# A two-layer hybrid backbone on one core: the opening of the first layer regrouped into quarters, with identity transposes in TensorE's early waits

## The chip, the cores and the metric

The kernel runs on one core of one Trainium2 chip. The metric is the device time of one execution in microseconds (us). A core has TensorE (PE; its weight loads are listed apart as PEld), VectorE (DVE), ScalarE (ACT), GpSimd (POOL) and SyncE (SP), each with an instruction queue of its own that it works off in order, and 16 DMA engines that move data between memory and the on-chip buffers.

## The reference

There are 1024 latent tokens and 256 context tokens of width 1024, and two layers. Each layer normalizes the tokens, scales and shifts them by a modulation that is computed from a conditioning vector (one for the latent, one for the context tokens), mixes them, and adds the gated result. Layer 0 mixes by windowed attention with sink logits, layer 1 by multi-head latent attention.

```python
def adaln(cond, w, bias):
    m = jax.nn.silu(cond) @ w + bias
    return jnp.split(m, 3, axis=-1)
...
        shift_x, scale_x, gate_x = adaln(c, ada_w[i], ada_b[i])
        shift_c, scale_c, gate_c = adaln(c_ctx, ada_w[i], ada_b[i])
        hx = rms_norm(x, norm_g[i]) * (1.0 + scale_x[:, None]) + shift_x[:, None]
        hc = rms_norm(ctx, norm_g[i]) * (1.0 + scale_c) + shift_c
...
        q, k, v, g = jnp.split(h @ w_in, [A_WIDTH, A_WIDTH + A_KV_WIDTH, A_WIDTH + 2 * A_KV_WIDTH], axis=-1)
...
        x = x + gate_x[:, None] * yx
        if need_ctx:
            ctx = ctx + gate_c * yc
    return rms_norm(x, final_g)
```

All of it is float32. In `adaln` the first third of the columns is the shift and the second the scale; the gates are computed elsewhere in the kernel.

## The kernel before

Most products are made from operands cut into a high part (rounded to the format in which TensorE streams fastest) and a low part (the rest). `mm3` (lines 124 to 128) adds three matmuls: high by high, low by high, high by low; the profile has them as L126, L127 and L128. `split` (lines 119 to 122) makes the parts: ScalarE copies the high one (L121), another engine subtracts (L122).

The tokens lie in ten row tiles of 128, two context and eight latent tiles, handled as five pairs of 256 tokens. The **opening** (lines 657 to 864) makes the modulated input `hT` of layer 0, which all later projections read, and the first product from it, the values `V`, whose weights are block 0 (`w0`, 1024 x 256). Then a loop over the other blocks of the input projection begins (line 869), in an order written out by hand (`in_order`), then the attention, then layer 1.

The steps of the opening, by function:

- `ada_load(h, k)` loads modulation weights, 128 rows of a 512-column half `h` of shift and of scale (0.52 MB), into one of six buffers; `ada_mm(h, k)` (L676) makes two matmuls of 512 columns from them, for shift and scale. Eight `k` make a half. `ada_cols(h)` copies the two sums out of the bank (L679), turns them into columns (L681), and `set_cols` (L168, L171) adds the biases and forms the columns `A` (scale) and `B` (shift).
- `x_load(i)` loads a row tile (0.52 MB) into one of **four** buffers `xs`. `norm(i)` sums its squares on ScalarE (L692) and has GpSimd form the inverse root (L693, L694); `scale(i)` multiplies the tile by it (L701 on VectorE, L699 on ScalarE).
- A **group** is a pair `p` and a quarter `b` of the 1024 columns; there are 20. `turn(g)` (L712) makes four 128x128 transposes into a bank. `h_part(g)` has VectorE scale and shift them out of it (L723, two of 128x256) and ScalarE round the high half (L724, 128x512); `h_low(g)` subtracts for the low half (L729, on GpSimd or VectorE). The scaled group lies in one of four buffers `hr` until then. `v_part(g)` makes the group's twelve value matmuls, and at a pair's last quarter takes the values out of the bank (L745, L747).
- `w0_load` and `w0_cut` load and split quarters of block 0 of the weights; `fetch` (L288) does so for later blocks. `load_small` loads the identity `ident`, the modulation biases, the norm gains and the sink logits on ScalarE's queue, and VectorE negates the sinks (L151). All other loads are issued by SyncE.

Groups go in the order quarters 0 and 1 of pairs 0 and 1, then their quarters 2 and 3, then four quarters of each of pairs 2 to 4. The opening's order on each engine is the planner's, which sorts by priority and may let an instruction of a later stage go first; the stage behind it (`in_order`) is in program order.

Behind the opening, `ada_vec` computes the rest of the modulation on VectorE (L342, L344), step by step in the projection loop, and TensorE sums it over the rows (L355).

Of the kernel before, what the change touches and what calls it, by code (L numbers as in the profile page):

```python
# [9 lines left out]
F32 = mybir.dt.float32  # L10
# [8 lines left out]
D = 1024  # L19
# [8 lines left out]
F_KB = 66  # L28
# [31 lines left out]
def kernel(ctx: ExitStack, tc: tile.TileContext, t, out, dbg=None):  # L60
# [93 lines left out]
    class AdaLN:  # L154
# [8 lines left out]
        def set_cols(self, mt, what, h):  # L163

            l, j0 = self.layer, 8 * what + 4 * h
            bias = adab[:, l, j0 : j0 + 4].unsqueeze(2).to_broadcast([128, 4, 2])
            dst = (self.A if what else self.B)[:, 4 * h : 4 * h + 4]
            nc.vector.tensor_add(dst, mt, bias)  # L168
            if what:
                g = ng[:, l, 4 * h : 4 * h + 4].unsqueeze(2).to_broadcast([128, 4, 2])  # L170
                nc.vector.scalar_tensor_tensor(dst, dst, 1.0, g, ALU.add, ALU.mult)  # L171
# [108 lines left out]
    def fetch(bi):  # L280
# [9 lines left out]
        def cut(i):  # L290
            ks = slice(2 * i, 2 * i + 2)
            split(wt[bi][:, 0, ks, :], wt[bi][:, 1, ks, :], got[i], nc.gpsimd)
# [364 lines left out]
    awr = Ring(F, [0, 4, 8, 12, 16, 20], 1024)  # L657
    xs = Ring(F, [24, 28, 32, 36], 1024)
    w0r = Ring(F, [40, 42], 512)
    am = f_at(48, 512)  # L660
    junk = f_at(50, 512).bitcast(BF16)
    hr = Ring(F, [44, 46, 40, 42], 512)
    PA, PM = PB[:, 6, :], PB[:, 7, :]
    parts = [(p, b) for h in range(2) for p in range(2) for b in (2 * h, 2 * h + 1)]
    parts += [(p, b) for p in range(2, NP) for b in range(4)]
    NG = len(parts)
    aw, xn, hs, w0 = {}, {}, {}, {}

    def ada_load(h, k):
        aw[h, k] = shp(awr.next(), 2, 512)  # L670
        src = t["ada_w"][0, k * 128 : k * 128 + 128, 0 : 2 * D].rearrange("p (a c) -> p a c", a=2)
        load(out=aw[h, k], in_=src[:, :, h * 512 : h * 512 + 512])

    def ada_mm(h, k):
        for a in range(2):
            nc.tensor.matmul(PA[32 * a : 32 * a + 2], sc[:, k, :], aw[h, k][:, a, :], start=k == 0, stop=k == 7)  # L676

    def ada_cols(h):
        nc.scalar.copy(am[0:34], PA[0:34])  # L679
        for j in range(4):  # L680
            nc.tensor.transpose(PM[:, 34 * j : 34 * j + 34], am[0:34, j * 128 : j * 128 + 128], ident[0:34, 0:34])  # L681
        m = shp(PM, 4, 34)
        ada0.set_cols(m[:, :, 32:34], 1, h)
        ada0.set_cols(m[:, :, 0:2], 0, h)
# [962 lines left out]
```

## Time and profile before

| what | value |
|---|---|
| time, median of three runs | 1561.43 us (1560.34 to 1561.45) |
| time of the profiled execution | 1563.35 us |
| its span, first to last instruction | 1561.6 us |
| mean granted TensorE clock | 0.989 of full speed |
| moved by DMA | 178.91 MB, mean 115 GB/s |
| DMA share in the first ten microseconds / the next twenty | 0.72 / 1.05 |
| chain that ended last, share of PE | 86% |

A row of a group of instructions names the line in the kernel, the engine, the operation, what is written and read with its shape, how many there were, and times. A float32 matmul of the modulation counts as two records. Durations of matmuls overlap, so the distance from one start to the next says what one costs. In a list of waits the columns are total, times and longest in us. A row of one line of the kernel has the shortest, median and longest duration in ns, then the first and last start in us.

### The profile page before, as it was taken

The numbers are of one execution on the slowest core, as the hardware profiler recorded it, in microseconds if no ns is written. First come the engines' busy times: TensorE is split into PE (matmuls) and PEld (weight loads), VectorE is DVE, ScalarE is ACT, GpSimd is POOL, SyncE is SP. The second block draws the span as 40 slices with busy tenths as digits, with TensorE's granted clock in tenths as the row PEclk, the third lists the DMA queues.
The fourth block names the chain that finished last, engine by engine and source line by source line (L and its number), as shares of the span: only waits on it lengthen the run. The fifth ranks groups of instructions, "written<-read, shape, count | busy, mean of one in ns | idle before, by whom it ended". The sixth has DMA issues, their size and how long they took to land.

```text
span 1561.6 us, 24793 instructions
## 1 busy us (share of the span) xinstructions
PE 1513.9 (97%) x9074; PEld 1207.1 (77%) x9074; DVE 953.2 (61%) x1859; ACT 714.1 (46%) x1369; POOL 816.3 (52%) x764
## 2 busy tenths in 40 slices
PE   6899999999999999998999999999999999999998
PEld 2797888687888888887988788766876875885686
DVE  2666968827767787777826301556566566566644
ACT  2512212219877777776623332244443443453422
POOL 2652545417544443344517351278789789699200
PEclk8899999999999999999999999999999999999999
DMA  8425544474433322326304851402122112211442
GB/s 303 178 92 186 198 140 169 151 223 138 121 109 99 97 89 88 95 68 203 109 9 138 295 155 63 124 9 58 45 68 65 51 46 74 58 44 45 142 155 81
DMA packets 123986, 178.91 MB, mean 115 GB/s; under 512 B 11724, under 2 KB 72268, under 8 KB 123864
## 3 DMA queue, kind: packets, MB, share of 16 engines
q1 hardware_dynamic: 119032, 170.27, 34.8%
q10 hardware_dynamic: 4832, 7.06, 1.3%
q8 instruction: 71, 1.16, 0.3%
q14 instruction: 51, 0.42, 0.1%
HBM read 131.13 MB, written 46.15 MB: 114 GB/s over the span
## 4 chain that ended last, share of the span: by engine, by line
PE 86%; DMA 3%; DVE 3%; ACT 3%; issue 2%; POOL 2%; SPq 0%; POOLq 0%; DVEq 0%; ACTq 0%
PE PB L126 14%; PE PB L127 14%; PE PB L128 14%; PE PB L1345 12%; PE PB L1368 9%; PE PB L572 5%; PE PB L1311 5%; PE PB L562 4%; PE PB L532 2%; PE PB L533 2%; DMA arena_f<-a_w_in 1%; PE PB L1379 1%; DVE arena_f L344 1%; DMA arena_f<-b_w_in 1%; PE PB L355 1%
## 5 line engine op out<-in xcount | busy, mean ns | idle before, releaser
L126 PE MATMUL PB<-arena_r 128*128 128x512 f32 (+2 forms) x1312 | 477.2, 364 | 4.9 <-ACT arena_r L205 2.1
L127 PE MATMUL PB<-arena_r 128*128 128x512 f32 (+2 forms) x1312 | 470.0, 358 | 2.9 <-POOL arena_r L729 2.0
L128 PE MATMUL PB<-arena_r 128*128 128x512 f32 (+2 forms) x1312 | 469.8, 358 | 0.2 <-DVE arena_r L122 0.2
L126 PEld LDWEIGHTS PB<-arena_r 128*128 128x128 f32 x1312 | 250.6, 191 | 58.9 <-issue 16.0
L1361 POOL TENSOR_TENSOR arena_f<-arena_f 128x1024 f32<-128x1024 f32 x120 | 285.9, 2382 | 8.2
L127 PEld LDWEIGHTS PB<-arena_r 128*128 128x128 f32 x1312 | 250.4, 191 | 37.3 <-POOL arena_r L729 2.6
L128 PEld LDWEIGHTS PB<-arena_r 128*128 128x128 f32 x1312 | 250.2, 191 | 35.6 <-DVE arena_r L122 0.4
L1345 PE MATMUL PB<-arena_r 64*128 64x512 f32 (+1 forms) x1600 | 225.8, 395 | 0.0
L122 POOL TENSOR_TENSOR arena_r<-arena_f,arena_r 128x512 fp32r<-128x512 f32 x98 | 134.7, 1388 | 164.4 <-ACT arena_r L121 164.3
L1317 DVE TENSOR_REDUCE krF<-PB 128x1 f32<-128x512 f32 (+1 forms) x264 | 167.3, 678 | 79.6 <-PE PB L1311 79.6
L1355 ACT ACTIVATE arena_f<-PB 128x1024 f32<-128x1024 f32 x160 | 164.5, 1028 | 111.4 <-PE PB L1345 84.6
L122 DVE TENSOR_TENSOR arena_r<-PB,arena_r 128x512 fp32r<-128x512 f32 (+2 forms) x215 | 140.4, 664 | 92.4 <-ACT arena_r L121 91.5
L1345 PEld LDWEIGHTS PB<-arena_r 64*128 64x128 f32 (+1 forms) x1600 | 174.0, 185 | 17.2 <-issue 5.2
L121 ACT CAST arena_r<-PB 128x512 fp32r<-128x512 f32 (+2 forms) x215 | 120.4, 565 | 120.6 <-PE PB L128 74.0
L539 DVE CUSTOM_DVE_ANT_0 arena_f<-PB,arena_f,small 128x256 f32<-128x256 f32 (+1 forms) x288 | 145.4, 524 | 46.1 <-PE PB L533 39.4
L1368 PE MATMUL PB<-arena_f 128*64 128x512 f32 x640 | 145.9, 595 | 0.0
L545 ACT ACTIVATE arena_f<-arena_f,small 128x640 f32<-128x640 f32 (+2 forms) x160 | 118.9, 744 | 28.8 <-DVE small L539 27.9
L572 PE MATMUL PB<-arena_r 128*128 128x512 f32 x336 | 120.7, 435 | 4.2 <-ACT arena_f L583 4.1
L344 DVE SCALAR_TENSOR_TENSOR arena_f<-arena_f,small 128x512 f32<-128x512 f32 x98 | 112.9, 1198 | 11.6 <-DMA arena_f<-ada_w 11.3
L1311 PE MATMUL PB<-arena_r 64*128 64x512 f32 (+1 forms) x768 | 109.5, 354 | 0.7 <-DVE arena_r L122 0.7
L1368 PEld LDWEIGHTS PB<-arena_f 128*64 128x64 f32 x640 | 44.0, 137 | 79.6 <-issue 79.0
L562 PE MATMUL PB<-ident,arena_f 128*128 128x128 f32 x672 | 104.8, 273 | 0.5 <-ACT arena_f L545 0.3
(165 smaller groups left out, 1869.6 us busy)
## 6 DMA issues: line engine op xcount, KB each, us to landing
arena_r<-q_d SPq DMA_DIRECT2D x160, 128.0 KB, 3.0
arena_f<-ada_w SPq DMA_DIRECT2D x64, 256.0 KB, 3.6
arena_f<-a_w_in SPq DMA_DIRECT2D x40, 256.0 KB, 3.8
arena_f<-ada_w SPq DMA_DIRECT2D x16, 512.0 KB, 5.0
arena_f<-x SPq DMA_DIRECT2D x16, 512.0 KB, 6.3
q_d<-arena_f SPq DMA_DIRECT2D x16, 512.0 KB, 2.6
qn_d<-arena_f SPq DMA_DIRECT2D x16, 512.0 KB, 5.1
arena_r<-qn_d SPq DMA_DIRECT2D x16, 512.0 KB
```

The costliest lines, as they stand in the source:

```text
L122: (lo_eng or nc.vector).tensor_sub(lo, src, hi.bitcast(F32))
L126: nc.tensor.matmul(o, ah, bh, start=first, stop=False)
L127: nc.tensor.matmul(o, al, bh, start=False, stop=False)
L128: nc.tensor.matmul(o, ah, bl, start=False, stop=last)
L562: nc.tensor.transpose(pt[:, h, :], self.Ps[h][:, ci * 128 : ci * 128 + 128], ident)
L572: nc.tensor.matmul(self.pv, V[:, self.chunks[ci], self.g, :], PT[:, s], start=ci == 0 and s == 0, stop=ci == self.m - 1 and s == 1,)
L1311: nc.tensor.matmul(bank[:, o : o + n], self.q[r, s, bs], k[r, 0, n0 : n0 + n], start=s == 0, stop=s == 2)
L1317: nc.vector.reduce_max(self.mxp[:, e, b : b + 1, i], bank[:, 0:n], AX.X)
L1345: nc.tensor.matmul(PB[:, b + e, :], k[r, s, cs], q[r, sq], start=i == 0, stop=i == 4)
L1355: nc.scalar.activation(E, PB[:, b : b + 2, :], AF.Exp)
L1361: eng.tensor_add(acc, acc, E)
L1368: nc.tensor.matmul(PB[r, 7, :], Vq[:, c, h, :], E[:, e], start=c == 0, stop=c == NT - 1)
```

## The change

The opening is written anew; what it computes stays.

- **Quarters.** The modulation comes in four quarters of 256 columns. `ada_load(q, kk)` loads 256 rows at a time, as two transfers of 0.26 MB (shift and scale), into four buffers. `ada_mm(q, kk)` makes four matmuls of 256 columns; the two row halves go to separate rows of the bank. `ada_copy` takes 98 rows out, and `ada_cols` turns and adds the halves by one matmul for each 128 columns with `sel`, the sum of two pieces of the identity. `set_cols` gets a width, here 2.
- **All row tiles kept.** Each pair has its own buffer of 8 KB a partition, so `x_load` needs none to come free. The buffer of the scaled groups, `hr`, has two places in place of four. The float32 arena grows by 1 KB a partition.
- **Order.** Groups go quarter by quarter over the pairs: quarters 0 and 1 of pairs 0 to 2, then of pairs 3 and 4, then quarters 2 and 3 of all. A pair has a value bank of its own (0 to 4), and groups are turned alternately in banks 5 and 7. `v_part` makes the eight matmuls with the high half of the input first and the four with the low half last. The whole opening stands in a manual schedule: on each engine, program order.
- **Engines.** The mean of squares moves to VectorE; the high halves of two groups and of one weight quarter are cast by GpSimd; other halves are shared out anew.
- **Identity turns.** `keep_up(n)` has TensorE transpose the identity `n` times into bank 2, which is not in use then: 16 at first, 5 after each of three modulation steps, 4, 16, 5, and 3 after each of two steps, 62 in all.

Left out below are the removed lines, which stand above, and the plain changes to `set_cols` and `fetch`.

```diff
@@ -654,214 +655,251 @@
+    awr = Ring(F, [0, 10, 14, 18], 1024)
+    hr = Ring(F, [62, 64], 512)
+    am = f_at(66, 256)
+    PA = PB[:, 6, :]
+    sel = sm(34)
+    aw, xn, hs, w0, tbank = {}, {}, {}, {}, {}
+    def ada_load(q, kk):
+        aw[q, kk] = shp(awr.next(), 2, 2, 256)
+        src = t["ada_w"][0, kk * 256 : kk * 256 + 256, 0 : 2 * D].rearrange("(k p) (a c) -> p k a c", p=128, a=2)
         for a in range(2):
+            load(out=aw[q, kk][:, :, a], in_=src[:, :, a, q * 256 : q * 256 + 256])
+    def ada_mm(q, kk):
+        for k in range(2):
+            for a in range(2):
+                r = 64 * k + 32 * a
+                nc.tensor.matmul(
+                    PA[r : r + 2, 0:256], sc[:, 2 * kk + k, :], aw[q, kk][:, k, a], start=kk == 0, stop=kk == 3
+                )
+    def ada_copy():
+        nc.scalar.copy(am[0:98], PA[0:98, 0:256])
+    def ada_cols(q):
+        for j in range(2):
+            o = PA[:, 256 + 34 * j : 290 + 34 * j]
+            nc.tensor.matmul(o, am[0:98, j * 128 : j * 128 + 128], sel[0:98], start=True, stop=True)
+        m = shp(PA[:, 256:512], 2, 34)
+        ada0.set_cols(m[:, :, 32:34], 1, q, 2)
+        ada0.set_cols(m[:, :, 0:2], 0, q, 2)
+    def x_load(p):
+        xn[p] = [f_at(22 + 8 * p, 2, 1024), sm_ring(), sm_ring()]
+        src = t["ctx"] if p == 0 else t["x"][(2 * p - 2) * 128 : 2 * p * 128, :]
+        for j in range(2):
+            load(out=xn[p][0][:, j], in_=src[j * 128 : j * 128 + 128, :])
+    def square(p):
+        junk = V[:, 8:10].rearrange("p a b c -> p (a b c)") if p > 2 else PB[:, 3:5, :].rearrange("p a b -> p (a b)")
+        for j in range(2):
+            nc.scalar.activation(junk, xn[p][0][:, j], AF.Square, accum_out=xn[p][1][:, j : j + 1])
+    def norm(p):
+        _, sq, st = xn[p]
+        nc.vector.tensor_scalar(st[:, 0:2], sq[:, 0:2], 1.0 / D, EPS, ALU.mult, ALU.add)
+        nc.gpsimd.tensor_tensor(st[:, 2:4], st[:, 0:2], mhalf.to_broadcast([128, 2]), ALU.pow)
+    def scale(p, j, eng):
+        x, r = xn[p][0][:, j], xn[p][2][:, 2 + j : 3 + j]
         if eng is nc.scalar:
+            nc.scalar.activation(x, x, AF.Copy, scale=r)
         else:
+            eng.tensor_scalar_mul(x, x, r)
+    def turn(p, b, bank):
+        tbank[p, b] = ps = shp(PB[:, bank, :], 2, 256)
         for kk in range(2):
             for j in range(2):
                 c0 = (2 * b + kk) * 128
+                nc.tensor.transpose(ps[:, kk, j * 128 : j * 128 + 128], xn[p][0][:, j, c0 : c0 + 128], ident)
+    def h_part(p, b, hi=nc.scalar.copy):
         w = 1 if p == 0 else 0
+        ps, h = tbank[p, b], shp(hr.next(), 2, 256)
         for kk in range(2):
             k = 2 * b + kk
             sa, sb = ada0.A[:, k, w : w + 1], ada0.B[:, k, w : w + 1]
+            nc.vector.tensor_scalar(h[:, kk], ps[:, kk], sa, sb, ALU.mult, ALU.add)
         ks = slice(2 * b, 2 * b + 2)
+        hi(hT[p][:, 0, ks, :], h)
+        hs[p, b] = h
+    def h_low(p, b, eng=nc.gpsimd):
+        ks = slice(2 * b, 2 * b + 2)
+        eng.tensor_sub(hT[p][:, 1, ks, :], hs[p, b], hT[p][:, 0, ks, :].bitcast(F32))
+    def v_part(p, b):
         h, W = hT[p], wt[0]
         for j in range(2):
             js = slice(j * 128, j * 128 + 128)
+            o = PB[:, p, j * 256 : j * 256 + 256]
             for k in (2 * b, 2 * b + 1):
+                for s in range(2):
+                    nc.tensor.matmul(o, h[:, 0, k, js], W[:, s, k, :], start=k == j == s == 0, stop=False)
+        for j in range(2):
+            js = slice(j * 128, j * 128 + 128)
+            o = PB[:, p, j * 256 : j * 256 + 256]
+            for k in (2 * b, 2 * b + 1):
+                nc.tensor.matmul(o, h[:, 1, k, js], W[:, 0, k, :], start=False, stop=j == 1 and k == 7)
+    def v_out(p):
+        o = PB[:, p, :].rearrange("p (j h d) -> p j h d", j=2, h=4)
+        vs = V[:, 2 * p : 2 * p + 2]
+        for j in range(2):
+            nc.scalar.copy(vs[:, j, :, 0:64], o[:, j])
+        for j in range(2):
+            nc.vector.tensor_sub(vs[:, j, :, 64:128], o[:, j], vs[:, j, :, 0:64].bitcast(F32))
     wt[0] = r_at(wst[0], 2, 8, 256)
     def w0_load(i):
+        w0[i] = f_at((58, 60, 4, 6)[i], 2, 256)
         load(out=w0[i], in_=w_in[256 * i : 256 * i + 256, 1280:1536].rearrange("(k p) n -> p k n", p=128))
+    def w0_cut(i, top=nc.scalar.copy):
+        hi, lo = (wt[0][:, s, 2 * i : 2 * i + 2, :] for s in range(2))
+        top(hi, w0[i])
+        nc.gpsimd.tensor_sub(lo, w0[i], hi.bitcast(F32))
+    groups = [(p, q) for q in range(2) for p in range(3)] + [(3, 0), (3, 1), (4, 0), (4, 1)]
+    groups += [(p, q) for q in range(2, 4) for p in range(NP)]
+    NG = len(groups)
+    def make(i):
+        if i < NG:
+            turn(*groups[i], (5, 7)[i % 2])
+            h_part(*groups[i], nc.gpsimd.tensor_copy if i == 3 else nc.scalar.copy)
+        if i < 9:
+            h_low(*groups[i])
+        elif 10 < i <= NG:
+            h_low(*groups[i - 1], nc.vector if i % 2 or i in (14, 16) else nc.gpsimd)
+        if i == 9:
+            h_low(*groups[i])
+    def keep_up(n):
+        for _ in range(n):
+            nc.tensor.transpose(PB[:, 2, 0:128], ident, ident)
+    opening = tc.manual_schedule()
+    opening.__enter__()
+    nc.vector.memset(PA[0:98], 0.0)
+    x_load(0)
     load_small()
+    for kk in range(4):
+        ada_load(0, kk)
+    w0_load(0)
+    nc.vector.tensor_add(sel[0:98], ident[0:98, 0:34], ident[0:98, 64:98])
     x_load(1)
+    x_load(2)
     w0_load(1)
+    square(0)
+    norm(0)
+    for j in range(2):
+        scale(0, j, nc.vector)
+    keep_up(16)
+    for kk in range(3):
+        ada_mm(0, kk)
+        keep_up(5)
+    turn(0, 0, 5)
     ada_mm(0, 3)
+    keep_up(4)
+    ada_copy()
+    ada_cols(0)
+    keep_up(16)
+    for kk in range(4):
+        ada_load(1, kk)
+    x_load(3)
+    w0_load(2)
+    w0_load(3)
+    w0_cut(0, nc.gpsimd.tensor_copy)
+    h_part(0, 0, nc.gpsimd.tensor_copy)
+    square(1)
+    norm(1)
+    h_low(0, 0, nc.vector)
+    for j in range(2):
+        scale(1, j, nc.vector)
+    v_part(0, 0)
+    turn(1, 0, 7)
+    keep_up(5)
+    square(2)
+    norm(2)
+    h_part(1, 0)
+    scale(2, 0, nc.vector)
+    scale(2, 1, nc.scalar)
     w0_cut(1)
+    for kk in range(2):
+        ada_mm(1, kk)
+        keep_up(3)
+    h_low(1, 0, nc.vector)
+    v_part(1, 0)
+    turn(2, 0, 5)
+    ada_mm(1, 2)
+    h_part(2, 0)
+    h_low(2, 0, nc.vector)
+    ada_mm(1, 3)
+    ada_copy()
+    turn(0, 1, 7)
+    ada_cols(1)
+    x_load(4)
+    for kk in range(4):
+        ada_load(2, kk)
+    v_part(2, 0)
+    turn(1, 1, 5)
+    h_part(0, 1, nc.gpsimd.tensor_copy)
+    square(3)
+    h_low(0, 1, nc.vector)
     norm(3)
+    h_part(1, 1)
+    h_low(1, 1)
+    for i in range(3, NG):
+        p, q = groups[i]
+        if i > 7:
+            make(i + 2)
+        if i == 3:
+            scale(3, 0, nc.vector)
+            scale(3, 1, nc.scalar)
+        v_part(p, q)
+        if i < 8:
+            make(i + 2)
+        if i == 3:
+            square(4)
             norm(4)
+        if i == 5:
+            scale(4, 0, nc.vector)
+            scale(4, 1, nc.scalar)
+            ada_mm(2, 0)
+            ada_mm(2, 1)
+            w0_cut(2)
+        if i == 6:
+            ada_mm(2, 2)
+            ada_mm(2, 3)
+            ada_copy()
+            w0_cut(3)
+        if i == 7:
+            ada_cols(2)
+            for kk in range(4):
+                ada_load(3, kk)
+        if i == 9:
             fetch(1)
+        if i in (9, 11):
+            ada_mm(3, i - 9)
+            ada_mm(3, i - 8)
+        if i == 11:
+            ada_copy()
             load(out=cosa, in_=t["cos_a"])
             load(out=sina, in_=t["sin_a"])
+        if i == 12:
+            ada_cols(3)
+        if i > 15:
+            v_out(p - 1)
+        if i in (12, 14, 16):
+            next_item()
+    v_out(4)
+    opening.__exit__(None, None, None)
     started = {0, 1}
     in_order = tc.manual_schedule()
```

More of the change, by code (lines that the diff above doesn't have):

```diff
@@ L27 @@
 R_KB = 152
-F_KB = 66
+F_KB = 67
 NEG = -1e30
@@ L278, in next_item, with fetch @@
             fn()
-    def fetch(bi):
+    def fetch(bi, eng=nc.gpsimd):
         wt[bi] = r_at(wst[bi % 2], 2, 8, 256)
@@ L291, in cut @@
             ks = slice(2 * i, 2 * i + 2)
[L292 removed]
+            split(wt[bi][:, 0, ks, :], wt[bi][:, 1, ks, :], got[i], eng)
         def second():
@@ L652, in steps @@
             next(g, None)
[L657 to L674, printed above, removed]
-        for a in range(2):
[L676 to L684, printed above, removed]
```

149 lines of the change are left out of this document (6 added, 143 removed).

## The prediction

> **What bounds the kernel now.** I read first the page's engine table, then busy time by stage, the waits of the opening, and the timeline of single engines.
>
> ```profile
> span 1561.6 us, 24793 instructions
> PE 1513.9 (97%) x9074; PEld 1207.1 (77%) x9074; DVE 953.2 (61%) x1859; ACT 714.1 (46%) x1369; POOL 816.3 (52%) x764
> ```
>
> TensorE bounds the kernel as a whole. By stage (columns: stretch, length, then busy time of each engine, granted clock, DMA share, GB/s):
>
> ```profile
> 0.00:86.40 86.40, 66.84 (x394) 46.41 (x395) 39.80 (x79) 34.34 (x63) 39.11 (x48) 0.88 0.62 218
> 86.40:1561.60 1475.20, 1447.03 (x8683) 1160.72 (x8681) 913.36 (x1780) 679.74 (x1306) 777.15 (x716) 0.99 0.35 109
> 24.20:31.00 6.80, 5.86 (x21) 3.52 (x22) 3.84 (x5) 2.23 (x4) 4.23 (x5) 0.51 1.05 387
> 48.60:56.00 7.40, 6.26 (x31) 5.97 (x32) 6.03 (x10) 4.88 (x8) 7.23 (x8) 0.56 0.41 154
> 71.60:75.60 4.00, 4.00 (x22) 4.00 (x23) 2.58 (x7) 1.56 (x4) 1.48 (x2) 0.57 0.00 0
> 65.00:70.00 5.00, 2.78 (x22) 2.38 (x21) 2.87 (x4) 3.41 (x7) 3.04 (x5) 1.00 0.88 323
> 103.60:109.30 5.70, 5.70 (x27) 4.70 (x26) 5.65 (x9) 0.62 (x1) 3.44 (x3) 1.00 0.24 95
> ...
> 86.47 0.65 ACT L745 CAST arena_r<-PB 128x256 fp32r<-128x256 f32 x2 [4.59 <-PE PB L128]
> ```
>
> The last row is ScalarE taking out the last value tile: the opening, the only part changed, ends on TensorE at 86.4 us. In it TensorE idles 19.6 us and runs in three spells at about half clock. Behind it the array is 98% busy, so what the opening saves should arrive at the end.
>
> ```profile
> SPq L688 <- PE PB L712: 8.6, 3, 4.1
> ...
> DVE arena_f L701 <- POOL small L694: 13.6, 5, 7.2
> ACT arena_f L692 <- DMA arena_f<-x: 9.7, 3, 5.8
> PE PB L676 <- DMA arena_f<-ada_w: 5.9, 2, 5.6
> ...
> 37.22 5.37 SPq L688 DMA_DIRECT2D arena_f<-x  x4
> 59.74 1.43 SPq L688 DMA_DIRECT2D arena_f<-x  x2
> ```
>
> This is one chain: row tiles 4 to 9 are asked for only at 37.22 and 59.74, since SyncE waits for transposes (L712) to free the four x buffers; ScalarE waits for those tiles, then GpSimd's power and VectorE's scaling (L701), then TensorE's transposes.
>
> **What the opening's work costs at full speed.**
>
> ```profile
> 31.78 1.03 PE L676 MATMUL PB<-arena_f,small 128*2 128x512 f32 x4
> 32.74 0.44 PE L712 MATMUL PB<-ident,arena_f 128*128 128x128 f32 x2
> ...
> 61.67 0.60 PE L712 MATMUL PB<-ident,arena_f 128*128 128x128 f32 x4
> 63.45 0.46 PEld L712 LDWEIGHTS PB<-ident,arena_f 128*128 128x128 f32 x4
> 63.55 0.60 PE L712 MATMUL PB<-ident,arena_f 128*128 128x128 f32 x4
> ...
> 14.05 1.81 PE L676 MATMUL PB<-arena_f,small 128*2 128x512 f32 x4
> 15.80 1.54 PE L712 MATMUL PB<-ident,arena_f 128*128 128x128 f32 x6
> 17.27 2.87 PE L676 MATMUL PB<-arena_f,small 128*2 128x512 f32 x12
> ...
> 74.12 0.80 PEld L712 LDWEIGHTS PB<-ident,arena_f 128*128 128x128 f32 x4
> ```
>
> A group (four transposes and twelve value matmuls) takes 63.55 - 61.67 = 1.88 us; 20 groups make 37.6. A modulation step takes 32.74 - 31.78 = 0.96, at low clock 15.80 - 14.05 = 1.75; 16 steps make 15.4. Together 53 us of 86.4. A transpose costs 0.46/4 = 0.115 us, at low clock 0.20.
>
> **The change, part by part.** Prices of the other engines:
>
> ```profile
> L692 ACT ACTIVATE arena_f<-arena_f x10: 1052/1056/1059, 10.8 to 67.1; 128x1024 bf16<-128x1024 f32 x10
> L701 DVE TENSOR_SCALAR arena_f<-arena_f,small x8: 744/754/1756, 12.9 to 67.1; 128x1024 f32<-128x1024 f32 x8
> L723 DVE TENSOR_SCALAR arena_f<-PB,small x40: 529/536/545, 23.1 to 80.2; 128x256 f32<-128x256 f32 x40
> L724 ACT CAST arena_r<-arena_f x20: 602/618/634, 24.1 to 81.2; 128x512 fp32r<-128x512 f32 x20
> L729 POOL TENSOR_TENSOR arena_r<-arena_f,arena_r x16: 1272/1294/1747, 24.8 to 82.0; 128x512 fp32r<-128x512 f32 x16
> L640 POOL CAST arena_r<-arena_f x8: 607/616/618, 354.4 to 366.7; 128x512 fp32r<-128x512 f32 x8
> ...
> 21.60 0.57 ACT L679 COPY arena_f<-PB 34x512 f32<-34x512 f32 x1
> 23.11 1.45 DVE L723 TENSOR_SCALAR arena_f<-PB,small 128x256 f32<-128x256 f32 x3
> 24.81 0.58 PE L126 MATMUL PB<-arena_r 128*128 128x256 f32 x1
> ...
> 1.17 4.34 DMA arena_f<-ada_w
> ```
>
> *Loads.* Bytes are the same, 14.7 MB or 38 us at the 387 GB/s of a row above; 46 issues replace 30, at most 1.43/2 = 0.7 us each on SyncE (59.74 row), 33 us in all, under the transfers. The first 0.52 MB (1.17 to 5.5 us) is 1.35 us of bytes, so about 3.0 us is start and landing. All x buffers exist, so x waits for nobody; modulation pieces wait for four buffers. The order is tile pair 0 (1.05 MB), quarter 0 (2.10), weights, pairs 1 and 2, weights, quarter 1, pair 3, weights, pair 4, quarter 2. With 1 us more for pieces that wait for earlier transfers (an estimate; SyncE in the rows above also pauses), landing is 1.2 + 3.0 + 1 + bytes/387: quarter 0 at 5.2 + 8.1 = 13.3, quarter 1 (7.9 MB) at 25.5, pair 4 (10.5 MB) at 32.3.
>
> *Quarter steps.* Sixteen steps of four 256-column matmuls stream the same columns as before, so 0.96 each; the shape is not in the trace. Below it I put half (four column strips overlapping twice as far), above it 1.75, the low-clock price. I take 0.96, the nearest row.
>
> *First group.* Last step of quarter 0 to 14.2; from the copy's start to the first scaling was 23.11 - 21.60 = 1.5, so 15.7; two scalings 1.0; the high half now a GpSimd cast, 0.62: value matmuls start at about 17.5, against 24.81. VectorE's queue is now strictly as written, and this gains a wait:
>
> ```profile
> 11.10 0.17 DVE L151 TENSOR_SCALAR small<-small 128x16 f32<-128x16 f32 x1 [9.45 <-DMA small<-a_sink]
> 71.22 0.86 DVE L342 TENSOR_SCALAR arena_f<-arena_f,small 128x512 f32<-128x512 f32 x1
> 75.15 0.49 DVE L342 TENSOR_SCALAR arena_f<-arena_f,small 128x512 f32<-128x512 f32 x1 [1.29 <-PE PB L712]
> 78.40 1.41 DVE L344 SCALAR_TENSOR_TENSOR arena_f<-arena_f,small 128x512 f32<-128x512 f32 x2
> 92.85 0.69 DVE L122 TENSOR_TENSOR arena_f<-PB,arena_f 128x512 fp32r<-128x512 f32 x1 [4.94 <-ACT arena_f L121]
> ```
>
> Behind the sink values (here until 11.1) stand the selector, the mean and both scalings of pair 0, for which TensorE's first turn waits. Freed at 11, two at 0.75 end by 13, ahead of quarter 0; the cover is 0.3 us, and each later microsecond would count in full.
>
> *Quarter 1.* Its last step ends at 27.3 with groups (1,0) and (2,0) between; + 1.5 + 1.0 + 0.62 gives (0,1) at about 30.5.
>
> *From there on* TensorE has 17 groups, 32.0; eight steps, 7.7; two column turns, 0.8: 40.5, to 71.0. For waits I add 4: pair 4's two squares hold ScalarE 2.5 us and VectorE's mean waits behind them with the next groups' scalings queued after it (about 2.8), and half of one low-clock spell like 48.60 to 56.00 (1.2). VectorE needs 2 x 0.5 + 0.69 (a 128x512 subtraction, 92.85 row) = 1.7 us a group there, under TensorE's 1.88. The opening ends at 75.0. The waits could be 0 or 8: 71 to 79.
>
> *Identity turns.* 62 transposes are 7.1 us at 0.115. Thirty-one stand ahead of quarter 0's last step, four under the copy, 16 between 15.2 (the column turn) and 17.5, 11 inside the wait for quarter 1. So I count them at nothing; without that cover the sixteen delay group 0 by up to 16 x 0.20 - 2.3 = 0.9. Their use: above, about 3.6 us of work (13.7 to 17.3) went at half speed before the steps ran fast.
>
> *Moved work.* The later stage's first VectorE sums ran early, in gaps of the opening (rows from 71.22 to 78.40); now they follow it, 0.86 + 0.49 + 1.41 = 2.8 us, beside the first projection, where VectorE idled 4.94 (92.85). Price 0; 2.8 if it can't be taken up (103.60 to 109.30 shows VectorE full).
>
> **Sum.** 86.4 - 75.0 = 11.4 us off. The profiled execution took 1563.35 us, 1.75 beyond its span; the median of the runs shown is 1561.43, which I subtract from: 1550.0.
>
> **Rivals.** *The identity turns do not raise the clock* (the change does not do what it says). For: in 13.7 to 17.3 real steps stand beside the transposes, so no row shows transposes alone raising it. Against: steps lie among them here too. At low clock from about 5.5 (the identity is asked for before the first modulation piece, which lands then): 16 x 0.20, three times (1.75 + 5 x 0.20), a turn of 0.8, and the last step 1.75 end at 19.5, not 14.2. Five us late, little of it caught up before quarter 1's chain: opening at 80, 1555. The Trainium skill, "TensorE: Matmul & The Clock Gate", section on the PE-mode transpose, says the full clock does not engage for transpose mode; by that rule this rival's time holds, and no run here has shown it yet.
>
> *In-order queues serialize the groups; slower.* If each of groups 3 to 9 and the three before pays its whole chain, 0.46 + 1.0 + 0.62 + 1.29 (GpSimd's low half) + 0.48 for the last four matmuls = 3.85 instead of 1.88, ten groups cost 19.7 more; less the 4 counted, the opening ends at 90.7: 1566. It decides once waits exceed my sum by 11.4. For: ScalarE and VectorE now hold squares, means and scalings of later pairs ahead of nearer groups, and the h ring shrinks from four buffers to two, so a scaling waits for the low half two groups back. Against: groups are prepared two ahead, that low half is then a whole group old, and nothing waits for x buffers.
>
> *Steps overlap and all waits vanish*: 71.0 less 8 x 0.48 is 67.2: 1542.
>
> *VectorE gives it back* behind the opening, 2.8: 1553.
>
> **Chances.** Forecast 0.60, clock 0.17, serialized 0.11, overlap 0.07, given back 0.05. The range 1543 to 1558 leaves out the serialized case and most of the overlap case and takes in the 71 to 79 bounds and the clock case. A measurement here tells about 0.2% (3 us) from no change. Faster by more: nearly all of forecast, overlap and given back, and most of the clock case, 0.86; within it, the clock case's and serialized case's near ends, 0.06; slower, the rest of the serialized case, 0.08.
>
> **What would show it.** First value matmul near 17.5 and quarter 1's columns near 28; the last value tile taken out near 75, not 86.4; granted clock near 1 from 9 us on; x loads asked for with no wait on transposes; VectorE not waiting on ScalarE's squares for more than a few us. The prediction is wrong if the opening's end moves less than 6 us, or moves and the end of the kernel does not follow.

## The result, and the profile after

| what | before | after |
|---|---|---|
| time, median (runs) | 1561.39 us on the same chip | 1545.84 us (1544.44 to 1547.34) |
| ratio after to before | | 0.9902, interval 0.9885 to 0.9919 |
| time of the profiled execution | 1563.35 us | 1544.44 us |
| its span | 1561.6 us | 1542.7 us |
| its mean granted clock | 0.989 | 0.998 |
| last value tile taken out (end of the opening) | 86.47 us | 71.44 us |

The kernel became 1.0% faster: 15.6 us in the medians, where 11.4 were forecast. The forecast time of 1550.0 lies 4 us too high; the measured one lies inside the range of 1543 to 1558.

The first rows of the page, then busy time by stage (columns as before: stretch, length, busy time of PE, PEld, DVE, ACT and POOL, granted clock, DMA share, GB/s), of the kernel after:

```profile
span 1542.7 us, 25091 instructions
PE 1508.9 (98%) x9208; PEld 1210.6 (78%) x9208; DVE 954.7 (62%) x1875; ACT 713.9 (46%) x1369; POOL 805.5 (52%) x747
...
0.00:72.00 72.00, 65.29 (x538) 52.63 (x539) 39.17 (x91) 34.89 (x65) 29.68 (x31) 1.00 0.78 261
19.95:71.40 51.45, 49.61 (x442) 42.48 (x443) 34.49 (x72) 27.04 (x51) 26.23 (x23) 1.00 0.75 245
32.20:71.44 39.24, 38.53 (x343) 34.23 (x344) 26.94 (x56) 20.18 (x39) 22.99 (x19) 1.00 0.65 205
```

Before, TensorE idled 19.6 us in 86.4 and its clock was 0.88 in the mean. Now it idles 6.7 us in 72, some 4.9 of them before 20 us; from the first value matmuls on it idles 51.45 - 49.61 = 1.8 us, and from the first group of the second quarter on 0.7. No five-microsecond row from 15 to 80 us has a clock under 1.00: the three spells at half clock are gone.

The timeline of TensorE in the same kernel (start, duration, line, operands, count, idle time ahead and what ended it), and one row each of ScalarE and SyncE:

```profile
2.85 3.67 PE L785 MATMUL PB<-ident 128*128 128x128 f32 x16 [2.85 <-DMA ident<-ident]
...
10.00 1.33 PE L785 MATMUL PB<-ident 128*128 128x128 f32 x5
11.26 1.03 PE L675 MATMUL PB<-arena_f,small 128*2 128x256 f32 x8
12.22 1.33 PE L785 MATMUL PB<-ident 128*128 128x128 f32 x5
...
15.90 0.61 PE L675 MATMUL PB<-arena_f,small 128*2 128x256 f32 x8
17.50 1.94 PE L785 MATMUL PB<-ident 128*128 128x128 f32 x16
19.95 1.21 PE L742 MATMUL PB<-arena_r 128*128 128x256 f32 x8 [0.51 <-POOL arena_r L728]
25.15 1.19 PE L742 MATMUL PB<-arena_r 128*128 128x256 f32 x8
27.18 1.04 PE L675 MATMUL PB<-arena_f,small 128*2 128x256 f32 x16
28.16 0.66 PE L718 MATMUL PB<-ident,arena_f 128*128 128x128 f32 x4
32.20 1.21 PE L742 MATMUL PB<-arena_r 128*128 128x256 f32 x8 [0.36 <-POOL arena_r L728]
...
71.44 0.65 ACT L753 CAST arena_r<-PB 128x256 fp32r<-128x256 f32 x2 [0.82 <-PE PB L747]
25.04 2.56 SPq L694 DMA_DIRECT2D arena_f<-x  x2
```

L785 are the identity turns, L675 the modulation steps, L718 the turns of groups, L742 and L747 the value matmuls (high halves, then the low one). Group (0,0) starts at 19.95, group (1,0) at 25.15, the second quarter's first group (0,1) at 32.20. The last pair's tiles are asked for at 25.04, where SyncE's row names no wait. Two steps now take 28.16 - 27.18 = 0.98 us, which is 0.49 each: half the price that the prediction took. The early ones are twice as slow, 12.22 - 11.26 = 0.96. (The mean clock reads 1.00 in these stretches too; durations show the half speed ahead of 15 us, the clock column doesn't.)

**What lies behind the opening.** One line of the projection loop (the rotation, L430 before and L431 after; shortest, median, longest ns, first and last start), one of the attention (L532 and L533), and two windows:

```profile
L430 DVE TENSOR_TENSOR arena_f<-PB,arena_f x20: 691/692/693, 97.7 to 291.8; 128x512 f32<-128x512 f32 x20
L532 PE MATMUL PB<-arena_r x288: 277/282/446, 342.2 to 701.3; 128*128 128x256 f32 x132, 128*128 128x384 f32 x12
310.00:320.00 10.00, 10.00 (x35) 6.51 (x35) 5.89 (x9) 1.11 (x2) 0.00 (x0) 0.83 0.86 257
```

for the kernel before, and for the kernel after:

```profile
L431 DVE TENSOR_TENSOR arena_f<-PB,arena_f x20: 691/692/693, 82.1 to 276.1; 128x512 f32<-128x512 f32 x20
L533 PE MATMUL PB<-arena_r x288: 277/282/446, 323.9 to 682.7; 128*128 128x256 f32 x132, 128*128 128x384 f32 x12
294.30:304.30 10.00, 10.00 (x43) 7.44 (x42) 4.95 (x8) 1.20 (x2) 0.00 (x0) 1.00 0.95 297
```

The saving of 15.0 us reaches the loop as 97.7 - 82.1 = 15.6 and leaves it as 291.8 - 276.1 = 15.7: nothing is given back to the VectorE sums that moved behind the opening. Between the last rotation and the attention it grows to 342.2 - 323.9 = 18.3. There TensorE waits for the last projection weights, 2.3 us before and 1.1 after, and before it then ran at a granted clock of 0.83 for ten microseconds, after at 1.00. This is no accident of the two executions. In all three traces with the old opening (before, and its two variants with early tiles below) TensorE waits 2.3 to 2.5 us there, the clock falls, and from the start of the last rotation to the start of the attention it takes 50.4 to 50.7 us. In all eleven with the new opening it waits 0.5 to 1.3, the clock stays, and it takes 46.9 to 47.9. So some 2.5 to 3.8 us more go with the new opening, which the prediction did not have. SyncE asks for the last weights 10.4 to 10.5 us behind the start of the last rotation in both kernels; from there to ScalarE's cast of them it takes 5.6 us in the kernel before and 4.5 in the kernel after. Why they come sooner was not followed up.

The profiled executions end 18.9 us apart, the medians only 15.6, and 17.0 when the kernel after ran again on another chip (below). Executions of one kernel range over 3 us, so the medians can't tell the two parts of the saving apart; the traces do.

### The profile page after: what moved, and what is told of

It reads as the page before. It is cut to its first block, busy times and chain, and to the rows that moved or that the text cites. A ratio compares the mean times of both kernels' runs of the same rounds, so it can differ in the third digit from the quotient of the medians.

```text
span 1542.7 us, 25091 instructions
## 1 busy us (share of the span) xinstructions
PE 1508.9 (98%) x9208; PEld 1210.6 (78%) x9208; DVE 954.7 (62%) x1875; ACT 713.9 (46%) x1369; POOL 805.5 (52%) x747
## 4 chain that ended last, share of the span: by engine, by line
PE 85%; DVE 4%; POOL 3%; ACT 3%; issue 2%; DMA 2%; POOLq 0%; SPq 0%; DVEq 0%; ACTq 0%
PE PB L126 13%; PE PB L127 13%; PE PB L128 13%; PE PB L1383 12%; PE PB L1406 9%; PE PB L573 5%; PE PB L1349 5%; PE PB L563 4%; PE PB L533 2%; PE PB L534 2%; PE PB L1417 1%; PE PB L742 1%; DVE arena_f L345 1%; ACT arena_f L584 1%; POOL arena_f L1141 1%
## 5 line engine op out<-in xcount | busy, mean ns | idle before, releaser
L126 PE MATMUL PB<-arena_r 128*128 128x512 f32 (+2 forms) x1232 | 450.6, 366 | 4.5 <-ACT arena_r L206 2.1
L127 PE MATMUL PB<-arena_r 128*128 128x512 f32 (+2 forms) x1232 | 445.2, 362 | 0.9 <-POOL arena_r L122 0.8
L128 PE MATMUL PB<-arena_r 128*128 128x512 f32 (+2 forms) x1232 | 445.1, 361 | 0.2 <-DVE arena_r L122 0.2
L126 PEld LDWEIGHTS PB<-arena_r 128*128 128x128 f32 x1232 | 233.0, 189 | 56.6 <-issue 14.3
L128 PEld LDWEIGHTS PB<-arena_r 128*128 128x128 f32 x1232 | 233.0, 189 | 35.4 <-DVE arena_r L122 0.4
L127 PEld LDWEIGHTS PB<-arena_r 128*128 128x128 f32 x1232 | 233.0, 189 | 34.1 <-POOL arena_r L122 1.8
L540 DVE CUSTOM_DVE_ANT_0 arena_f<-PB,arena_f,small 128x256 f32<-128x256 f32 (+1 forms) x288 | 145.4, 524 | 46.1 <-PE PB L534 39.4
```

The costliest lines, as they stand in the source:

```text
L126: nc.tensor.matmul(o, ah, bh, start=first, stop=False)
L127: nc.tensor.matmul(o, al, bh, start=False, stop=False)
L128: nc.tensor.matmul(o, ah, bl, start=False, stop=last)
```

## The experiments

In each diff `-` is the kernel that was edited. Times are medians, beside 1561 to 1562 us of the kernel before on the same chip.

**Are the identity turns worth anything?** Three kernels leave out all of them, the 35 ahead of quarter 0's copy, or the 27 behind it.

```diff
     def keep_up(n):
-        for _ in range(n):
-            nc.tensor.transpose(PB[:, 2, 0:128], ident, ident)
+        return
```

> All 62 identity turns left out; nothing else changes. In the profile of the changed kernel the opening ends on TensorE at 71.4 us; 15 turns stand between the steps of quarter 0 at low clock (9.0 to 16.5 us, 1.26 us for each five). Theory 'the turns hold the clock': quarter 0's steps end 2 to 3 us earlier, but the waits between 14 and 30 us bring low-clock spells, and the opening ends at 71 to 74, with granted clock or step durations at half speed somewhere between 17 and 30. Theory 'the turns only take time': no low-clock spell beyond the first, and the opening ends at 68 to 69.5.

```diff
-    keep_up(16)
     for kk in range(3):
         ada_mm(0, kk)
-        keep_up(5)
     turn(0, 0, 5)
     ada_mm(0, 3)
-    keep_up(4)
```

> The 35 turns up to quarter 0's copy left out, the later 27 (16, 5, 3 and 3) kept. Theory 'the early turns do not raise the clock' (the steps between 9.0 and 14.4 us ran at 0.96 us each although 16 turns had run from 2.85 to 6.5 without a gap): steps of quarter 0 end 2 to 3 us earlier, and the opening ends at 68.5 to 70. Theory 'they do bring the full clock forward': the first steps stay slow for longer, full speed comes later than 15 us, and the opening ends at 71 or later.

```diff
     ada_cols(0)
-    keep_up(16)
...
     turn(1, 0, 7)
-    keep_up(5)
...
         ada_mm(1, kk)
-        keep_up(3)
```

> The 27 turns behind quarter 0's copy left out (16, 5, 3 and 3), the first 35 kept. Theory 'the turns hold the clock': TensorE idles from 17.5 to about 20 us and in parts up to 30, the clock falls to half in one of these stretches, and the opening ends at 73 to 75. Theory 'the turns only take time': the opening ends at 71 to 71.5, or up to 0.5 earlier.

Without any: 1543.0 (ratio 0.9881, 0.9864 to 0.9897). Without the early ones: 1543.84 (0.9885, 0.987 to 0.990). Without the late ones: 1544.32 (0.9891, 0.9876 to 0.9906). All three stand at or a little below the kernel after. The timeline of TensorE without any turn, and its busy time by stage:

```profile
9.63 4.06 PE L675 MATMUL PB<-arena_f,small 128*2 128x256 f32 x22 [0.81 <-DMA arena_f<-ada_w]
14.20 0.61 PE L675 MATMUL PB<-arena_f,small 128*2 128x256 f32 x8
18.56 2.08 PE L742 MATMUL PB<-arena_r 128*128 128x256 f32 x8 [2.60 <-POOL arena_r L728]
22.50 2.17 PE L675 MATMUL PB<-arena_f,small 128*2 128x256 f32 x16
24.59 1.21 PE L742 MATMUL PB<-arena_r 128*128 128x256 f32 x8
...
20.00:25.00 5.00, 5.00 (x30) 2.62 (x30) 3.85 (x7) 2.63 (x5) 0.84 (x2) 0.62 1.11 352
```

The steps alone bring full speed by 14.20, earlier than in the kernel after (15.90), where fifteen turns, most of them at half speed, stood between them. A wait of 2.6 us follows, and the clock falls: 0.62 in the mean from 20 to 25 us, and the value matmuls of group (0,0) take 2.08 in place of 1.21; those of group (1,0), from 24.59 on, run at full speed again. With the late turns alone the clock holds there, so they do what they are for when the early ones are absent. With the early ones alone it held as well; TensorE without late turns:

```profile
20.29 1.22 PE L742 MATMUL PB<-arena_r 128*128 128x256 f32 x8 [2.29 <-POOL arena_r L728]
```

After 2.29 us of waiting the value matmuls still take 1.22. Whether the early turns or the shorter wait kept the clock there is not shown. Yet without any turns the opening ends at 70.87, 0.6 us earlier than with all of them: the spell of some five microseconds at half clock costs nothing that can be seen, since what stands behind it hangs on something else, as the next runs show.

**Can turns alone raise the clock?** One kernel makes the first 16 turns 40; another puts 20 real float32 matmuls of the identity in their place (40 records).

```diff
-    keep_up(16)
+    keep_up(40)
```

> The first 16 identity turns made 40, so that TensorE turns without a gap from about 3 us on. Theory 'turns raise the clock like any work': a turn costs 0.20 to 0.25 us for some 4 us and then 0.115, so the 40 end at about 9. Theory 'turns do not count for the clock': all 40 cost 0.20 or more and end at 11 us or later, and the steps behind them are slow at first.

```diff
-    keep_up(16)
+    for _ in range(20):
+        nc.tensor.matmul(PB[:, 2, 0:128], ident, ident, start=True, stop=True)
```

> The first 16 identity turns replaced by 20 float32 matmuls of the identity with itself (40 records; each product costs about as much as two turns). Both theories of the clock: real matmuls raise it after some 4 us, so the first records cost 0.21 and the later ones about half, they end at about 8 to 9, and the first steps of quarter 0 run at 0.49 us. If these stay slow too, the clock follows something else than the kind of work (time since the start, or the steps themselves).

One execution each: 1544.46 and 1549.28. Busy time by stage and two rows of TensorE with 40 turns:

```profile
5.00:7.00 2.00, 2.00 (x11) 2.00 (x11) 0.00 (x0) 1.12 (x2) 0.00 (x0) 1.00 1.02 366
8.00:9.80 1.80, 1.80 (x16) 1.78 (x15) 0.35 (x3) 0.43 (x2) 0.12 (x1) 1.00 1.05 318
...
2.60 7.42 PE L785 MATMUL PB<-ident 128*128 128x128 f32 x40 [2.60 <-DMA ident<-ident]
9.95 0.61 PE L675 MATMUL PB<-arena_f,small 128*2 128x256 f32 x8
```

Between 5 and 7 us eleven turns start in 2.0 us, 0.18 each; between 8 and 9.8 sixteen in 1.8, 0.11 each. Nothing else ran on TensorE. Transposes alone do raise the clock, some 5.5 us after they begin, and the 16 of the kernel after (3.3 us) are too few. The Trainium skill, "TensorE: Matmul & The Clock Gate", section on the PE-mode transpose, says that the full clock does not engage for transposes; here it did, and the measurement decides.

Rows of TensorE, its stage from 22 to 26 us, and rows of ScalarE and VectorE with real matmuls in front:

```profile
17.77 1.21 PE L742 MATMUL PB<-arena_r 128*128 128x256 f32 x8 [0.71 <-POOL arena_r L728]
20.29 0.74 PE L747 MATMUL PB<-arena_r 128*128 128x256 f32 x4 [1.31 <-DVE arena_r L733]
27.04 1.19 PE L742 MATMUL PB<-arena_r 128*128 128x256 f32 x8
...
22.00:26.00 4.00, 3.70 (x19) 2.04 (x19) 2.62 (x6) 2.71 (x6) 0.69 (x1) 0.57 1.01 325
...
17.02 1.03 ACT L699 ACTIVATE PB<-arena_f 128x1024 f32<-128x1024 f32 x1 [2.43 <-DMA arena_f<-x]
21.12 1.03 ACT L699 ACTIVATE PB<-arena_f 128x1024 f32<-128x1024 f32 x1 [1.68 <-DMA arena_f<-x]
...
19.48 0.17 DVE L703 TENSOR_SCALAR small<-small 128x2 f32<-128x2 f32 x1 [2.44 <-ACT PB L699]
```

Group (0,0) starts 2.2 us earlier than in the kernel after, and it doesn't help. ScalarE waits until 17.02 for a tile of pair 1; VectorE's mean (L703) waits for its squares, and the low half of group (0,0) (L733) stands behind that mean in VectorE's written order, so TensorE stops. Pair 2's tiles land later still here (21.12). The waits are followed by a spell at low clock (0.57 from 22 to 26 us): the two steps and eleven turns ahead of group (1,0) take from 22.79 to 27.04, 4.25 us, where they take 2.69 in the kernel after (22.46 to 25.15). Most of the 1.9 us by which group (1,0) comes later is this spell; whether the steps' weights were late too was not separated.

So a warm start is lost again where TensorE next waits, and it waits for row tiles and the squares behind them. In the kernel after the copy of quarter 0 and the first square of pair 1 follow each other without a wait:

```profile
16.61 0.37 ACT L680 COPY arena_f<-PB 98x256 f32<-98x256 f32 x1 [8.82 <-PE PB L675]
16.88 1.03 ACT L699 ACTIVATE PB<-arena_f 128x1024 f32<-128x1024 f32 x1
```

Without turns the copy comes at 14.91, 1.7 us earlier, but the square only at 16.37, since its tile is not there yet; with 40 turns at 14.81 and 16.20. The tiles land hardly earlier than the slow steps need them. The kernels that share the opening's second part show it (us; starts of L742 rows and of the last L753 row; time is the median, or the one execution):

```
kernel                      (1,0) starts   opening ends   difference     time
after                          25.15          71.44          46.29    1545.84
no turns                       24.59          70.87          46.28    1543.00
no early turns                 24.28          70.48          46.20    1543.84
no late turns                  24.70          70.80          46.10    1544.32
40 turns first                 25.01          71.19          46.18    1544.46
20 real matmuls first          27.04          73.21          46.17    1549.28
two strips (below)             27.12          76.22          49.10    1551.44
late row tiles (below)         24.58          77.53          52.95    1552.51
```

Whatever the turns do, the opening ends 46.1 to 46.3 us after group (1,0) starts, and with fewer turns that start comes up to 0.9 us sooner in this table (1.6 when the kernels ran again). But with all turns it was 25.15, 25.75 when the kernel ran again, and 24.58 in the run with late row tiles, so executions with the same turns differ as much. With real matmuls in front the opening ends 1.8 us later than in the kernel after and the one time is 3.4 us longer; what lies between was not followed up.

**How far do the column strips overlap?** The two row halves of a step go to the same rows of the bank, so a step uses two strips of the array instead of four; the values are the same sums.

```diff
-                r = 64 * k + 32 * a
+                r = 32 * a
...
-                    PA[r : r + 2, 0:256], sc[:, 2 * kk + k, :], aw[q, kk][:, k, a], start=kk == 0, stop=kk == 3
+                    PA[r : r + 2, 0:256], sc[:, 2 * kk + k, :], aw[q, kk][:, k, a], start=kk == k == 0, stop=kk == 3 and k == 1
...
-    nc.vector.tensor_add(sel[0:98], ident[0:98, 0:34], ident[0:98, 64:98])
+    nc.vector.tensor_copy(sel[0:98], ident[0:98, 0:34])
```

> The two row halves of a step are summed into the same two row strips as before, in place of four strips; the matmuls, their number and size stay, and the selector only copies. In the changed kernel a step takes 0.49 us at full clock (1.04 for the 16 records of two steps), in the kernel before 0.96. Theory 'four strips overlap twice as far': a step takes about 0.96 again, 1.75 at low clock; twelve steps behind the first quarter cost about 5 us more, quarter 0 up to 2 more; opening at 75 to 79. Theory 'a 256-column float32 matmul is cheaper for its own reason': steps stay at 0.49 and the opening at 71.4.

Measured: 1551.44 (0.993, 0.9916 to 0.9945), the opening ends at 76.22. TensorE in this kernel:

```profile
29.15 1.90 PE L675 MATMUL PB<-arena_f,small 128*2 128x256 f32 x16
30.98 0.66 PE L718 MATMUL PB<-ident,arena_f 128*128 128x128 f32 x4
```

Two steps cost 30.98 - 29.15 = 1.83, against 0.98 with four strips, for the same number of instructions, columns and bytes: 0.92 a step, near the price that the prediction took, and 0.49. Four strips overlap 1.87 times as far as two. (With two strips, matmuls that follow each other also add into the same rows of the bank; the run does not part this from the strips.) The Trainium skill, "TensorE: Matmul & The Clock Gate", section on packing small matmuls, gives 2.38 times for three column strips against none packed; the direction agrees, and a comparison without any packing was not run here. Undone, it costs 4.8 us of the opening: 2.0 ahead of group (1,0), 2.8 behind it, where ten steps of 0.43 more are partly taken up by waits that vanish.

**What are early row tiles worth, in the new order and in the old?** In the kernel after, pairs 3 and 4 are asked for behind the third quarter's weights:

```diff
-    x_load(3)
     w0_load(2)
...
-    x_load(4)
     for kk in range(4):
         ada_load(2, kk)
+    x_load(3)
+    x_load(4)
```

> The changed kernel with the loads of pairs 3 and 4 asked for behind quarter 2's pieces (which wait for quarter 1's steps), so about 10 and 5 us later than in the changed kernel (21.2 and 25.0 to 27.3). Theory 'early row tiles carry the opening': squares, scalings and transposes of pairs 3 and 4 come 5 to 9 us later, TensorE idles as long, and the opening ends at 75 to 80 in place of 71.4. Theory 'the tiles were early enough to spare': the opening ends at 71 to 72.5.

Measured: 1552.51 (0.995, 0.9931 to 0.9969), the opening ends at 77.53. ScalarE and TensorE:

```profile
35.32 1.06 ACT L699 ACTIVATE arena_r<-arena_f 128x1024 fp32r<-128x1024 f32 x1 [6.67 <-DMA arena_f<-x]
...
39.61 1.65 PE L742 MATMUL PB<-arena_r 128*128 128x256 f32 x6 [5.84 <-ACT arena_r L728]
```

Late tiles stop ScalarE for 6.67 us and TensorE for 5.84, and the opening ends 6.1 later. That is about the wait: the value matmuls behind it run at half clock (six in 1.65), and group (1,0) had started 0.6 earlier here.

Then the same in the kernel before: first with five more places in the tile ring, two of them taken from the modulation's, and tiles 4 to 9 asked for together.

```diff
-    awr = Ring(F, [0, 4, 8, 12, 16, 20], 1024)
-    xs = Ring(F, [24, 28, 32, 36], 1024)
+    awr = Ring(F, [0, 4, 8, 12], 1024)
+    xs = Ring(F, [24, 28, 32, 36, 16, 20, 52, 56, 60], 1024)
...
-    for i in range(4, 8):
+    for i in range(4, 10):
         x_load(i)
```

> The kernel before with nine buffers for row tiles in place of four (and four in place of six for modulation pieces), tiles 4 to 9 asked for together right behind the modulation pieces; halves, two strips, the planner's order and everything else stay. Theory 'waiting for row tiles was the larger part': the opening of the kernel before ends 6 to 10 us earlier than 86.4. Theory 'the halves and low-clock spells were': 0 to 4 us earlier.

1568.76 (1.0047), and inconclusive: with four buffers pieces 4 and 5 of the modulation overwrite pieces 0 and 1, whose steps stand later in the code, so part of the modulation is computed from other weights and the steps wait for loads that they should not wait for. The second version leaves the modulation's buffers alone.

```diff
-    xs = Ring(F, [24, 28, 32, 36], 1024)
+    xs = Ring(F, [24, 28, 32, 36, 52, 56, 60], 1024)
...
     for k in range(2, 6):
         ada_load(1, k)
+    for i in range(4, 7):
+        x_load(i)
     ada_cols(0)
...
-    for i in range(4, 8):
-        x_load(i)
+    x_load(7)
```

> The kernel before, with seven row-tile buffers instead of four and tiles 4 to 6 asked for as soon as the second half's first six modulation pieces are, tile 7 to 9 at their old places; the modulation stays in halves, no identity turns. Theory (tiles and quarters each carry a part, as late tiles cost 6 us in the kernel after): the opening ends 3 to 7 us earlier than 86.4, at 79 to 83, the time 1554 to 1558. Rival 1 (the quarters carry it all; early tiles only push the second half's modulation back, as the same bytes share the engines): the opening stays within 2 us of 86.4, 1560 to 1563. Rival 2 (the tiles carry it all): it ends below 76, under 1551.

Measured: 1555.25 (0.9956, 0.9939 to 0.9972). Busy time by stage, SyncE, TensorE and ScalarE of this kernel:

```profile
40.00:55.00 15.00, 11.79 (x65) 8.73 (x62) 6.49 (x16) 7.43 (x13) 7.52 (x9) 0.78 0.64 221
...
22.79 2.97 SPq L688 DMA_DIRECT2D arena_f<-x  x3
...
47.55 0.66 PE L712 MATMUL PB<-ident,arena_f 128*128 128x128 f32 x4 [1.49 <-DVE arena_f L723]
50.62 0.58 PE L127 MATMUL PB<-arena_r 128*128 128x256 f32 x1 [0.76 <-POOL arena_r L729]
...
80.75 0.65 ACT L745 CAST arena_r<-PB 128x256 fp32r<-128x256 f32 x2 [4.10 <-PE PB L128]
```

Three tiles are asked for at 22.79 instead of 37.22, the opening ends at 80.75 instead of 86.47, and the time falls by 6.4 us. Part of what is left stands where the halves meet: between 40 and 55 us TensorE idles 3.2 us at the turn from the first half to the second and then runs at half clock (its value matmuls there stand 0.21 apart, as they do at low clock, not 0.12). The tiles alone carry 5.7 of the 15.0; the other 9.3 came with quarters, strips and order together. (Here only three tiles come early, and tiles 7 to 9 wait as before, so this may be too little.)

**All, none, or only late turns, side by side on one chip.**

> The kernel after, unchanged, beside the two versions with fewer turns on one chip. Theory (the turns are worth nothing and cost about a microsecond): 1545 to 1546, 1 to 3 us above the other two. Rival (they make no difference): within 0.7 us of both.

> No identity turns at all. Theory: 1543 to 1544, below the kernel after by 1 to 3 us. Rival: equal within 0.7 us.

> Only the 27 later turns. Theory: it ends the opening first (70.5 against 70.9 without any and 71.4 with all), so 1543 to 1544, equal to no turns within 0.7 us and 1 to 2 below the kernel after. Rival: all three equal within 0.7 us, the scatter of the late low-clock spell being larger than what the turns change.

1544.67 (1543.96 to 1546.69), 1544.73 (1543.89 to 1545.55) and 1544.39 (1544.22 to 1545.99), beside 1561.66 of the kernel before: equal. The theory that the turns cost 1 to 3 us falls. Their openings end at 71.91, 70.35 and 70.80, so up to 1.6 us stay visible there, but executions of one kernel differ by 2 to 3 us behind it. Whether leaving the turns out gains the microsecond is not settled; that they bring none is. No version beat the kernel after by more than these runs can tell.

## Why the prediction came out as it did

**The place and the direction held.** The forecast was an opening that ends on TensorE at 75.0 and a saving that passes through the rest; it ended at 71.44, and 15.0 us of saving left the projection loop as 15.7. That it then grew to 18.3 was not in the prediction. The chain that the prediction read (buffers, late x loads, squares, power, scaling, transposes) is shown by both runs on row tiles: 6.1 us when it is put back, 5.7 when it alone is taken out of the kernel before.

**The mis-sized term is the quarter step.** The prediction put the sum from group (0,1) on at 32.0 + 7.7 + 0.8 + 4 = 44.5, from 30.5 to 75.0. It took 39.24, from 32.20:

```
term                         forecast   measured
start of (0,1)                 30.5       32.20
17 groups of 1.88              32.0       31.8 (63.78 - 61.91 = 1.87 a group in the rows below)
8 modulation steps              7.7        3.9 (8 x 0.49)
columns                         0.8        0.7 (0.37 and 0.36)
waits                           4          0.7 (39.24 - 38.53)
rest                            -          2.1
end                            75.0       71.44
```

```profile
61.91 0.60 PE L718 MATMUL PB<-ident,arena_f 128*128 128x128 f32 x4
62.27 1.20 PE L742 MATMUL PB<-arena_r 128*128 128x256 f32 x8
63.30 0.65 PE L747 MATMUL PB<-arena_r 128*128 128x256 f32 x4
63.78 0.60 PE L718 MATMUL PB<-ident,arena_f 128*128 128x128 f32 x4
```

These are two groups of the kernel after, one turn to the next. The price 0.96 came from "the nearest row", the 512-column steps of before; but in those two matmuls run beside each other, and in the new step four do. The prediction had named the lower bound, "four column strips overlapping twice as far", and the run with two strips shows that this bound was the truth. In the rest of 2.1, seven matmuls of the next stage that TensorE takes in between make 0.8; the remainder was not assigned. (It is a little larger still, as two of the 17 groups' transposes, 0.36 each, stood ahead of 32.20.)

So two terms were some 7 us too dear, and a later start and the rest nearly 4 too cheap. That the opening's end was missed by only 3.6 is in part luck.

**The waits were the second term.** The prediction wrote: "pair 4's two squares hold ScalarE 2.5 us and VectorE's mean waits behind them with the next groups' scalings queued after it (about 2.8)". VectorE in the kernel after:

```profile
38.34 0.17 DVE L703 TENSOR_SCALAR small<-small 128x2 f32<-128x2 f32 x1 [2.92 <-ACT arena_r L699]
38.42 1.90 DVE L726 TENSOR_SCALAR arena_f<-PB,small 128x256 f32<-128x256 f32 x4
```

The wait is there, 2.92 us, just as long as said. It hardly reached TensorE, which waits 0.18 us at 40.12: two groups were prepared ahead, four scalings follow at once (38.42), and the wait ends inside that lead. And since TensorE never stood still for long behind 20 us, no spell at low clock came either.

**The first group came later than forecast,** 19.95 and not 17.5, since the clock stayed low until about 15 us: the steps between the turns took 0.96 each, and the turns among them 0.25 each (1.26 for five). In the run with late row tiles, whose start is the same, the last step began at 14.37 and the first group at 18.42, so the moment also moves between executions. About the late clock the rival "the identity turns do not raise the clock" was half right: quarter 0's last step ended at 15.90 + 0.61 = 16.5, between the forecast's 14.2 and the rival's 19.5. But its price of five us was wrong, since the groups behind wait for row tiles and squares and not for group (0,0): without any turns the last step starts at 14.20 and the opening ends only 0.6 us earlier; with real matmuls in front group (0,0) starts 2.2 us earlier and it ends 1.8 us later. The identity turns were counted at nothing, and no run shows that they are worth more in the time; the full clock from 9 us on, which they were to bring, did not come.

**The other rivals.** The groups were not serialized (0.7 us of waits behind 32.2, where that case needed 11.4 more than the forecast's 4). VectorE gave nothing back: the sums moved behind the opening, and the loop's landmarks kept the saving of 15.6. "Steps overlap and all waits vanish", at 1542 and held for 0.07 likely, is the one that came nearest in its mechanism, with the first quarters 1.7 us later than it assumed, 0.7 of waits and 2.1 not assigned.

## What to carry to other kernels

A price taken from the nearest row must come from the same packing, not only the same number of columns: matmuls with few output rows cost by how many strips of the array run beside each other, and two starts in the trace give that price. Before paying for a warm clock, ask what the first warm work waits for next: if the group behind it hangs on a transfer, warming earlier only moves the wait, and the wait can lose the clock again. And when a change saves more at the end than at its own place, look at several traces of either kind before calling the difference scatter. A wait on an engine that prepares ahead counts only for what exceeds its lead.

## What the runs showed of the hardware

- Transposes alone brought TensorE from 0.18 to 0.11 us each, about 5.5 us after they began; 20 real float32 matmuls in the same place did it after some 3.3 us, in one execution of either kernel (rows of weight loads, 13 in 2.41 us from 3.67 on, then 10 in 1.20 from 5.89).
- A wait of about 2.5 us sometimes costs the clock and sometimes not: after 2.60 us without turns the clock fell (and after 2.64 when that kernel ran again), after 2.29 us without the late turns it did not.
- The column of the granted clock showed 1.00 in the first 15 us, where distances between starts show half speed. Early in an execution the distances are to be trusted.
